# A two-layer hybrid decoder on one core: two down units' inner activations made in the last up pass, another order of layer 0's down passes, and one more slot

## The chip, the core and the metric

The kernel runs on one core of a Trainium2 chip. The core has five engines that each follow an instruction queue of their own: TensorE (PE, matmuls), VectorE (DVE), ScalarE (ACT), GpSimd (POOL) and SyncE (SP, which here only starts transfers). Transfers run on 16 DMA engines. The metric is the time in device microseconds (us) of one execution; lower is better.

## The reference

Two layers (DEPTH 2) on 1024 tokens of width 1024, in float32. Each layer is a mixer and a channel sub-layer, both with adaptive norms whose shifts, scales and gates come from a product of one vector with a 1024x6144 matrix ("ada"):

```python
for l in range(DEPTH):
    mod = (cond @ w_ada[l] + b_ada[l])[:, None, :]
    shift_a, scale_a, gate_a, shift_f, scale_f, gate_f = jnp.split(mod, N_MOD, axis=-1)
    h = rms_norm(x) * (1.0 + scale_a) + shift_a
    mix = hybrid_mixer(h, cos, sin, ...)   # 4 heads of gated linear attention, 4 of latent attention with rotary keys
    x = x + gate_a * mix
    h = rms_norm(x) * (1.0 + scale_f) + shift_f
    x = x + gate_f * (jnp.square(jax.nn.relu(h @ w_mlp_up[l])) @ w_mlp_down[l])
```

The two products of the channel sub-layer are 1024x1024x4096 (up) and 1024x4096x1024 (down).

## The kernel before

**Precision.** Each float32 operand is split into a high part (a cast on ACT, or on DVE) and a low part (the difference), and each product is three matmuls, high x high, high x low and low x high: L161 to L163 in `mm3`. In the channel sub-layer each is 128x128 by 512 columns.

**Up and down as seven products.** Each of the two big products is cut into 2x2 blocks and done by Strassen's scheme with seven products instead of eight (`PRODUCTS`). A product names one or two weight blocks, one or two activation blocks, and the result blocks that it is added to. A *pass* is one product; a pass has eight *units* g = 0..7 of 24 matmuls. `UP_ORDER` and `DOWN_ORDER[l]` fix the order of the passes; layer 0's down order is 4, 7, 1, 5, 6, 2, 3, layer 1's is 4, 7, 1, 5, 3, 2, 6. Products 1, 6 and 7 have two weight blocks and two activation blocks. In the down products, 4 and 3 have one weight block and two activation blocks, 5 and 2 two weight blocks and one activation block.

**What a unit needs.** Its weights are loaded by SP (L292, and L298 for a second block), added on DVE if there are two blocks (L304), cast on ACT (L307), and the low part is taken on DVE (L308). Its inner activations are added on DVE (L1289, in place when the block is used for the last time), cast on ACT (L1291), and the low part is taken on DVE (L1292); this is `combine`, called by `down_moving`. So a unit with two blocks on both sides costs DVE four operations of 128x1024. In some units of layer 0 a step of the ada product of a later use runs on DVE too (L256, one load of 512 KB each). At the end of an up unit its result is added to one or two of the blocks C (L1338, on DVE, from PSUM); when a block of C is complete, ACT squares its positive part (L1311, L1312; block (0,1) in the first down pass). At the end of a down pass four banks are added to x, four or eight operations on DVE (L1417).

**Slots.** All large tiles, weights raw and split, inner activations, C, x and so on, are slots of 128x1024 float32 from one pool of `NSLOT` = 51. Free slots are handed out first in, first out. Weights are prepared two units ahead and loaded up to one or two further units ahead, while at least eight slots are free (`get`); inner activations are made one unit ahead in the first two down passes and two units ahead after (`moving_ahead`).

**Order on an engine.** A scheduler, which runs when the program is built, decides where each instruction stands in its engine's queue, with the order of the code as a preference. So an operation can stand well ahead of its place in the code when its inputs are there; each engine then follows its queue strictly.

**Rotary tables.** Cosines and sines (`cosT`, `sinT`, with the gains `grp`, three permanent tiles) are made in layer 0's mixer. In each layer `rope_tables` makes two slots of tables from them: six POOL multiplications (L577, L578, L580) and two on DVE (L579). In layer 1 this stands at the mixer's start, where the last down pass of layer 0 ends; L431 to L433 there are the norm of the first half of the tokens.

**Start.** The constants (L178), then 14 smaller transfers, all issued on ACT's queue, the last of them the gain rows (L204) that the transpose L208 needs; the condition vector and all of ada hang on it.

## Time and profile before

| | us |
|---|---|
| median of 3 runs | 2353.1 (2352.49 to 2366.69) |
| the profiled execution, its own time | 2356.47 |
| its span (first to last instruction) | 2354.4 |
| PE busy | 2236.2 (95%) |
| DVE busy | 1810.4 (77%) |
| ACT busy | 1141.1 (48%) |
| POOL busy | 453.5 (19%) |

"Span" is the time from the first instruction to the last; 2.1 us lie around it. Stretches are given in us from the span's start. The mean granted clock of PE was 0.982 of full speed. Layer 0's up passes end at 880.9, its down passes at 1214.4; layer 1's up passes end at about 2025.

### The profile page before, as it was taken

To read this page: it belongs to the slowest core of one execution; us is meant where nothing else is said; L and a number is where in the kernel's file an instruction comes from. 1 tells how busy PE (TensorE), PEld (TensorE's weight loads), DVE (VectorE), ACT (ScalarE), POOL (GpSimd) and SP (SyncE) were. 2 spreads that over 40 slices of the span, in tenths; PEclk is the share of its full clock that TensorE was granted. 3 is DMA by queue.
4 is the path that set the end of the run, shared out by engine and by line. 5 is a ranking of instruction groups with operands and counts; after the bars stand their busy time and mean duration, and the time that the engine had idled before them with its cause. 6 is when DMAs were issued, how large, how long until landed. Compare 5 with 4: busy or idle time off the path is not lost.

```text
span 2354.4 us, 30787 instructions
## 1 busy us (share of the span) xinstructions
PE 2236.2 (95%) x11784; PEld 1897.1 (81%) x11784; DVE 1810.4 (77%) x2453; ACT 1141.1 (48%) x1764; POOL 453.5 (19%) x326
## 2 busy tenths in 40 slices
PE   6999999899999998998989999899999999999999
PEld 4788888788788876887878889788888878887887
DVE  5897867857888888989995757786674767877894
ACT  3364746534732383433444556575366217733432
POOL 2452642420030000000063355333102000000000
PEclk8999999999999999999999999999999999999999
DMA  9633100136668655765641211003454564375562
GB/s 345 205 97 99 55 27 10 46 125 212 199 206 274 217 167 174 249 225 197 239 131 45 70 51 41 10 10 100 144 169 124 180 202 146 110 237 189 163 212 81
DMA packets 244855, 340.51 MB, mean 145 GB/s; under 512 B 11078, under 2 KB 166884, under 8 KB 244708
## 3 DMA queue, kind: packets, MB, share of 16 engines
q1 hardware_dynamic: 244160, 338.08, 44.2%
q8 instruction: 92, 1.51, 0.3%
q10 hardware_dynamic: 548, 0.48, 0.1%
q14 instruction: 55, 0.45, 0.1%
HBM read 317.54 MB, written 20.97 MB: 144 GB/s over the span
## 4 chain that ended last, share of the span: by engine, by line
PE 63%; DVE 12%; DMA 7%; ACT 2%; issue 2%; POOL 1%; SPq 0%; DVEq 0%; ACTq 0%; POOLq 0%
PE ps_m L162 8%; PE ps_m L163 7%; PE ps_m L161 7%; PE ps_s L162 5%; PE ps_s L163 5%; PE ps_s L161 5%; PE ps_g L163 4%; PE ps_g L162 4%; PE ps_g L161 4%; DMA s<-in_w_mlp_down_dram 3%; PE ps_x L163 2%; PE ps_x L162 2%; PE ps_x L161 2%; DMA s<-in_w_mlp_up_dram 2%; DMA s<-in_w_ada_dram 1%
## 5 line engine op out<-in xcount | busy, mean ns | idle before, releaser
L307 ACT CAST s<-s 128x1024 fp32r<-128x1024 f32 (+2 forms) x306 | 315.2, 1035 | 465.5 <-DVE s L304 275.7
L162 PE MATMUL ps_m<-s,s 128*128 128x512 f32 (+3 forms) x1084 | 411.1, 380 | 15.2 <-DVE s L1292 14.2
L308 POOL TENSOR_TENSOR s<-s,s 128x1024 fp32r<-128x1024 f32 (+2 forms) x90 | 222.7, 2481 | 1044.9 <-DVE s L307 524.1
L161 PE MATMUL ps_m<-s,s 128*128 128x512 f32 (+3 forms) x1084 | 408.6, 381 | 8.6 <-ACT s L1291 5.4
L163 PE MATMUL ps_m<-s,s 128*128 128x512 f32 (+3 forms) x1084 | 408.3, 377 | 0.2 <-DVE s L308 0.2
L308 DVE TENSOR_TENSOR s<-s,s 128x1024 fp32r<-128x1024 f32 (+1 forms) x224 | 272.5, 1227 | 55.6 <-ACT s L307 47.6
L161 PE MATMUL ps_s<-s,s 128*128 128x512 f32 (+5 forms) x800 | 306.4, 387 | 6.6 <-ACT s L724 6.1
L163 PE MATMUL ps_s<-s,s 128*128 128x512 f32 (+5 forms) x800 | 305.3, 383 | 1.5 <-DVE s L308 1.5
L162 PE MATMUL ps_s<-s,s 128*128 128x512 f32 (+5 forms) x800 | 305.2, 382 | 0.5 <-DVE s L748 0.5
L304 DVE TENSOR_TENSOR s<-s,s 128x1024 f32<-128x1024 f32 x160 | 196.9, 1233 | 122.1 <-DMA s<-in_w_mlp_up_dram 77.6
L162 PEld LDWEIGHTS ps_m<-s,s 128*128 128x128 f32 x1084 | 206.4, 190 | 55.9 <-DVE s L1292 17.7
L161 PEld LDWEIGHTS ps_m<-s,s 128*128 128x128 f32 x1084 | 205.6, 190 | 46.5 <-ACT s L1291 7.4
L1291 ACT CAST s<-s 128x1024 fp32r<-128x1024 f32 x140 | 146.7, 1051 | 192.8 <-DVE s L1289 57.2
L163 PEld LDWEIGHTS ps_m<-s,s 128*128 128x128 f32 x1084 | 206.0, 190 | 35.8 <-DVE s L308 0.6
L162 PE MATMUL ps_g<-s,s 128*128 128x512 f32 (+1 forms) x506 | 195.0, 386 | 1.6 <-DVE s L1292 1.6
L161 PE MATMUL ps_g<-s,s 128*128 128x512 f32 (+1 forms) x506 | 194.6, 388 | 0.8 <-DVE s L1338 0.8
L163 PE MATMUL ps_g<-s,s 128*128 128x512 f32 (+1 forms) x506 | 194.3, 387 | 0.8 <-DVE s L308 0.8
L1292 DVE TENSOR_TENSOR s<-s,s 128x1024 fp32r<-128x1024 f32 x140 | 173.5, 1244 | 13.8 <-ACT s L1291 10.8
L161 PEld LDWEIGHTS ps_s<-s,s 128*128 128x128 f32 x800 | 150.8, 189 | 37.0 <-ACT s L724 8.7
L163 PEld LDWEIGHTS ps_s<-s,s 128*128 128x128 f32 x800 | 151.4, 189 | 30.9 <-DVE s L308 1.9
L162 PEld LDWEIGHTS ps_s<-s,s 128*128 128x128 f32 x800 | 151.6, 190 | 27.6 <-DVE s L748 0.7
L162 PE MATMUL ps_x<-s,s 128*128 128x512 f32 (+3 forms) x362 | 124.1, 344 | 0.0
(332 smaller groups left out, 4412.6 us busy)
## 6 DMA issues: line engine op xcount, KB each, us to landing
s<-in_w_mlp_up_dram SPq DMA_DIRECT2D x192, 512.0 KB, 4.9
s<-in_w_mlp_down_dram SPq DMA_DIRECT2D x192, 512.0 KB, 4.3
s<-in_w_ada_dram SPq DMA_DIRECT2D x80, 512.0 KB, 4.8
s<-in_w_in_dram SPq DMA_DIRECT2D x48, 512.0 KB, 3.9
s<-in_w_ada_dram SPq DMA_DIRECT2D x32, 256.0 KB, 4.6
xd<-s SPq DMA_DIRECT2D x16, 512.0 KB, 6.1
s<-in_w_out_dram SPq DMA_DIRECT2D x16, 512.0 KB, 4.5
s<-xd SPq DMA_DIRECT2D x16, 512.0 KB, 3.5
```

Source lines behind the costliest of these rows:

```text
L161: PE.matmul(o, lh, rh, start=start, stop=False)
L162: PE.matmul(o, lh, rl, start=False, stop=False)
L163: PE.matmul(o, ll, rh, start=False, stop=stop)
L304: V.tensor_tensor(raw[:, :n], raw[:, :n], u.second[:, :n], op=ALU.add if u.sign > 0 else ALU.subtract)
L307: (V.tensor_copy if u.eng[-2] == "v" else S.copy)(R(u.hi[:, :n]), raw[:, :n])
L308: (V if u.eng[-1] == "v" else G).tensor_tensor(R(u.lo[:, :n]), raw[:, :n], u.hi[:, :n], op=ALU.subtract)
L1291: S.copy(R(hi), t)
L1292: V.tensor_tensor(R(lo), t, hi, op=ALU.subtract)
```

## The change

1. In the last of the seven up passes (n = 6), after unit 3, the inner activations of down unit 0 are made, and after unit 6 those of down unit 1, in both layers. `down_moving`, `steps` and `moving_ahead` move ahead of the up loop for this.
2. Layer 0's down order becomes 4, 6, 7, 1, 5, 2, 3. The third pass, too, now makes inner activations only one unit ahead and loads weights only one further unit ahead (n < 3 where it was n < 2), in both layers.
3. `NSLOT` becomes 52. Room for it comes from small tiles and from the three permanent rotary tiles: in layer 0 both layers' tables are made, those of layer 1 are stored to DRAM (two transfers of 512 KB), and layer 1 loads them (two more) in place of making them.
4. The constants are loaded in two parts with the causal mask going elsewhere, so ACT's queue issues two more transfers ahead of the gain rows.

```diff
-NSLOT = 51
+NSLOT = 52
-DOWN_ORDER = ((4, 7, 1, 5, 6, 2, 3), (4, 7, 1, 5, 3, 2, 6))
+DOWN_ORDER = ((4, 6, 7, 1, 5, 2, 3), (4, 7, 1, 5, 3, 2, 6))
...
-    cs = cp.tile([P, 416], F32, name="cs")
-    nc.scalar.dma_start(cs, cst[:, 0:416])
+    cs = cp.tile([P, 288], F32, name="cs")
+    nc.scalar.dma_start(cs[:, 0:128], cst[:, 0:128])
+    nc.scalar.dma_start(cs[:, 128:288], cst[:, 256:416])
...
     nc.scalar.dma_start(lvf[:, 0:320], cst[:, 416:736])
+    nc.scalar.dma_start(lvf[:, 320:448], cst[:, 128:256])
...
     def rope_angles():
-        ang = AR.alloc()
+        ang, trig = AR.alloc(), AR.alloc()
+        cosT, sinT, grp = trig[:, 0:256], trig[:, 256:512], trig[:, 512:768]
...
+        rope_tables(1, trig)
+        for i in range(2):
+            nc.sync.dma_start(rope_dram[i], rope_slots[i])
+        AR.free(*rope_slots)
+        rope_tables(0, trig)
+        AR.free(trig)
...
     def rope_tables(l, trig):
...
+            if trig is None:
+                nc.sync.dma_start(rope_slots[i], rope_dram[i])
+                continue
...
+        steps = [(m, g) for m in down_order for g in range(8)]
+        made = {}
+
+        def moving_ahead(i):
+            for j in steps[:i + 1]:
+                if j not in made:
+                    made[j] = down_moving(*j)
...
+                if n == 6 and g in (3, 6):
+                    moving_ahead(g // 6)
...
-                get(u, 2, 1 if n < 2 else 2)
-                moving_ahead(n * 8 + g + (1 if n < 2 else 2))
+                get(u, 2, 1 if n < 3 else 2)
+                moving_ahead(n * 8 + g + (1 if n < 3 else 2))
```

Line numbers shift with the change: L304, L308 become L307, L311; L256 becomes L259; L1289, L1292 become L1302, L1305; L1338 becomes L1370; L1417 becomes L1433; L431, L433 become L434, L436.

How it moves instructions, at three places. **First**, DVE where layer 0's up passes end. Before, the last two additions to C (the rows from PSUM tile ps_m at the head) stand ahead of everything that down unit 0 needs except its first addition; the low part of unit 0 is s_786, of unit 1 s_789, of unit 2 s_795, and the in-place additions (a tile added to itself) are for the pass of product 7:

```order
L1338 TENSOR_TENSOR s_747_7798<-s_747_7798,ps_m 128x512
L1338 TENSOR_TENSOR s_532_6077<-s_532_6077,ps_m 128x512
L1289 TENSOR_TENSOR s_494_5853<-s_494_5853,s_495_5855 128x1024
L308 TENSOR_TENSOR s_791_8211<-s_783_8170,s_790_8210 128x1024
L1292 TENSOR_TENSOR s_786_8175<-s_784_8172,s_785_8174 128x1024
L1289 TENSOR_TENSOR s_487_5809<-s_487_5809,s_488_5811 128x1024
L1292 TENSOR_TENSOR s_789_8181<-s_787_8178,s_788_8180 128x1024
L1289 TENSOR_TENSOR s_800_8257<-s_501_5897,s_553_6259 128x1024
L1292 TENSOR_TENSOR s_795_8219<-s_793_8216,s_794_8218 128x1024
```

Now unit 0's addition and low part (s_768, s_770) stand among the additions to C of the middle of that pass, with an in-place addition for product 7 between them:

```order
L1302 TENSOR_TENSOR s_768_7979<-s_481_5744,s_539_6112 128x1024
L1370 TENSOR_TENSOR s_725_7568<-s_725_7568,ps_s 128x512
L1370 TENSOR_TENSOR s_498_5837<-s_498_5837,ps_s 128x512
L1302 TENSOR_TENSOR s_481_5744<-s_481_5744,s_482_5746 128x1024
L1370 TENSOR_TENSOR s_725_7568<-s_725_7568,ps_g 128x512
L1370 TENSOR_TENSOR s_498_5837<-s_498_5837,ps_g 128x512
L1305 TENSOR_TENSOR s_770_7982<-s_768_7979,s_769_7981 128x1024
```

and behind the last two additions to C comes unit 2's low part (s_798), then unit 3's (s_805):

```order
L1370 TENSOR_TENSOR s_750_7780<-s_750_7780,ps_m 128x512
L1370 TENSOR_TENSOR s_535_6059<-s_535_6059,ps_m 128x512
L1302 TENSOR_TENSOR s_497_5835<-s_497_5835,s_498_5837 128x1024
L311 TENSOR_TENSOR s_794_8193<-s_792_8164,s_793_8192 128x1024
L1305 TENSOR_TENSOR s_798_8201<-s_796_8198,s_797_8200 128x1024
L259 SCALAR_TENSOR_TENSOR s_759_7896<-s_799_8230,cond,s_759_7896 128x1024
L1302 TENSOR_TENSOR s_803_8239<-s_504_5879,s_556_6241 128x1024
L311 TENSOR_TENSOR s_801_8234<-s_795_8196,s_800_8233 128x1024
L1302 TENSOR_TENSOR s_809_8296<-s_516_5933,s_568_6297 128x1024
L1302 TENSOR_TENSOR s_504_5879<-s_504_5879,s_505_5881 128x1024
L1305 TENSOR_TENSOR s_805_8242<-s_803_8239,s_804_8241 128x1024
```

Two units (four DVE operations) moved from behind the last addition to C to ahead of it; the in-place additions for product 7 stay on both sides.

**Second**, DVE in layer 0's second down pass. Before, this is product 7, whose activation additions were done in the first pass, so a unit has two weight rows (L304, L308) and one low part (L1292):

```order
L1292 TENSOR_TENSOR s_848_8547<-s_487_5809,s_847_8546 128x1024
L308 TENSOR_TENSOR s_840_8490<-s_837_8484,s_839_8489 128x1024
L304 TENSOR_TENSOR s_849_8574<-s_849_8574,s_850_8576 128x1024
L304 TENSOR_TENSOR s_843_8536<-s_843_8536,s_844_8538 128x1024
L1292 TENSOR_TENSOR s_854_8585<-s_494_5853,s_853_8584 128x1024
L304 TENSOR_TENSOR s_855_8612<-s_855_8612,s_856_8614 128x1024
L308 TENSOR_TENSOR s_846_8542<-s_843_8536,s_845_8541 128x1024
```

Now it is product 6. A unit has its own addition (s_858), its low part (s_860), two weight rows, and beside them an in-place addition (s_725) for product 3, the last pass:

```order
L1302 TENSOR_TENSOR s_858_8567<-s_551_6199,s_725_7568 128x1024
L311 TENSOR_TENSOR s_850_8525<-s_847_8519,s_849_8524 128x1024
L307 TENSOR_TENSOR s_854_8558<-s_854_8558,s_855_8560 128x1024
L1302 TENSOR_TENSOR s_725_7568<-s_725_7568,s_498_5837 128x1024
L1305 TENSOR_TENSOR s_860_8570<-s_858_8567,s_859_8569 128x1024
```

So a unit of the second pass has five rows on DVE where it had three.

**Third**, DVE where layer 0's last down pass ends and layer 1's mixer starts. Before, the two rotary rows (L579) stand between the norm and the additions that empty the last pass's banks:

```order
L433 SCALAR_TENSOR_TENSOR s_1124_10246<-tmp,mod,s_1124_10246 128x512
L433 SCALAR_TENSOR_TENSOR s_1125_10251<-tmp,mod,s_1125_10251 128x512
L579 SCALAR_TENSOR_TENSOR s_1181_10808<-sinT,grp 128x8x32 x2
L1417 SCALAR_TENSOR_TENSOR s_994_9411<-ps_m,mod,s_994_9411 128x512
L1417 SCALAR_TENSOR_TENSOR s_941_9073<-ps_m,mod,s_941_9073 128x512
```

Now nothing stands between; one more weight cast (L310) stands among the norm's rows, some way ahead:

```order
L434 SCALAR_TENSOR_TENSOR tmp<-s_832_8396,mod,tmp 128x512
L436 SCALAR_TENSOR_TENSOR s_1127_10228<-tmp,mod,s_1127_10228 128x512
L436 SCALAR_TENSOR_TENSOR s_1128_10233<-tmp,mod,s_1128_10233 128x512
L1433 SCALAR_TENSOR_TENSOR s_1053_9713<-ps_m,mod,s_1053_9713 128x512
L1433 SCALAR_TENSOR_TENSOR s_889_8729<-ps_m,mod,s_889_8729 128x512
```

Two rows have gone from ahead of the additions; POOL's six rows of layer 1's tables have gone too and stand in layer 0's mixer, beside layer 0's own six.

## Rows read from the trace of the kernel before

**Rows 1.** The page, busy time of each engine (share of the span, instructions).
```profile
PE 2236.2 (95%) x11784; PEld 1897.1 (81%) x11784; DVE 1810.4 (77%) x2453; ACT 1141.1 (48%) x1764; POOL 453.5 (19%) x326
```

**Rows 2.** Windows: start:end, length, busy PE PEld DVE ACT POOL, PEclk, DMA.
```profile
680.00:720.00 40.00, 40.00 (x178) 33.14 (x177) 35.80 (x43) 8.43 (x8) 5.70 (x3) 1.00 0.77 244
880.00:920.00 40.00, 31.30 (x128) 24.56 (x127) 33.72 (x38) 18.84 (x19) 0.00 (x0) 0.87 0.39 131
1080.00:1120.00 40.00, 34.71 (x144) 27.91 (x142) 38.48 (x37) 15.84 (x16) 0.00 (x0) 0.91 0.59 203
1200.00:1240.00 40.00, 33.52 (x212) 30.75 (x211) 32.99 (x31) 16.50 (x23) 23.12 (x12) 0.91 0.44 141
2120.00:2160.00 40.00, 35.16 (x147) 28.61 (x146) 31.00 (x29) 15.86 (x16) 0.00 (x0) 0.91 0.58 199
```

**Rows 3.** Waits in 870:930: who waited for whom, total us, times, longest.
```profile
PE ps_m L161 <- ACT s L1291: 4.7, 1, 4.7
...
PE ps_m L162 <- DVE s L1292: 2.6, 1, 2.6
...
PE ps_m L161 <- DVE s L1338: 1.4, 1, 1.4
```

**Rows 4.** DVE's timeline at the turn: start, us, operation, xcount [idle before].
```profile
881.17 2.35 DVE L1289 TENSOR_TENSOR s<-s,s 128x1024 f32<-128x1024 f32 x2
...
886.91 1.27 DVE L1338 TENSOR_TENSOR s<-s,ps_m 128x512 f32<-128x512 f32 x2
...
889.25 1.21 DVE L308 TENSOR_TENSOR s<-s,s 128x1024 fp32r<-128x1024 f32 x1
890.38 1.21 DVE L1292 TENSOR_TENSOR s<-s,s 128x1024 fp32r<-128x1024 f32 x1
```

**Rows 5.** DVE by line in 881:1214: xcount | busy us, mean ns | idle before.
```profile
L304 DVE TENSOR_TENSOR s<-s,s 128x1024 f32<-128x1024 f32 x40 | 48.7, 1222 | 11.5 <-DMA s<-in_w_mlp_down_dram 10.4 <-issue 0.8
...
L256 DVE SCALAR_TENSOR_TENSOR s<-s,cond,s 128x1024 f32<-128x1024 f32 x15 | 19.2, 1283 | 12.7 <-DMA s<-in_w_ada_dram 12.7
```

**Rows 6.** Waits in 1030:1130, the largest of PE.
```profile
PE ps_m L162 <- DVE s L1292: 5.4, 3, 4.6
```

**Rows 7.** Waits in 1190:1225, the only one of PE.
```profile
PE ps_m L609 <- ACT s L404: 6.5, 1, 6.5
```

**Rows 8.** DVE's timeline where layer 1's mixer starts.
```profile
1197.59 5.07 DVE L431 SCALAR_TENSOR_TENSOR tmp<-s,mod,tmp 128x512 f32<-128x512 f32 x3
...
1203.90 0.74 DVE L431 SCALAR_TENSOR_TENSOR tmp<-s,mod,tmp 128x512 f32<-128x512 f32 x1
...
1217.64 1.80 DVE L579 SCALAR_TENSOR_TENSOR s<-sinT,grp 128x256 f32<-128x256 f32 x2
1219.37 2.71 DVE L1417 SCALAR_TENSOR_TENSOR s<-ps_m,mod,s 128x512 f32<-128x512 f32 x4
```

**Rows 9.** POOL's timeline at the same place, first and last of four table operations.
```profile
1194.32 1.07 POOL L577 TENSOR_TENSOR s<-cosT,grp 128x256 f32<-128x256 f32 x1
...
1198.12 1.18 POOL L578 TENSOR_TENSOR s<-cosT,grp 128x256 f32<-128x256 f32 x1
```

**Rows 10.** The start, timeline of ACT's queue of transfers (ACTq).
```profile
0.77 0.39 ACTq L178 DMA_DIRECT2D cs<-in_cst_dram  x1
...
13.13 0.91 ACTq L204 DMA_DIRECT2D tmp<-in_k_norm_nope_dram  x2
```

**Rows 11.** The start, timeline of PE: the transpose that waits for the gain rows.
```profile
16.23 0.45 PE L208 MATMUL ps_x<-cs,tmp 128*128 128x128 f32 x1 [5.62 <-DMA tmp<-in_k_norm_nope_dram]
```

**Rows 12.** POOL's timeline in layer 0's mixer: last table, first operation that uses them.
```profile
117.30 0.73 POOL L578 TENSOR_TENSOR s<-cosT,grp 128x256 f32<-128x256 f32 x1
122.84 0.61 POOL L881 COPY s<-s 128x128 f32<-128x128 f32 x1 [4.82 <-DVE s L865]
```

**Rows 13.** Layer 1's down passes: waits in 2050:2135, the largest for a transfer.
```profile
DVE s L304 <- DMA s<-in_w_mlp_down_dram: 10.9, 5, 5.2
```

**Rows 14.** SP's own waits in 2040:2140, the longest.
```profile
SPq L292 <- PE ps_s L163: 35.4, 6, 11.8
```

More of the change, by code (lines that the diff above doesn't have):

```diff
@@ L176, in hybrid_kernel @@
     S.preload_act_table_set("natural_log_exp_and_others")
-    cs = cp.tile([P, 416], F32, name="cs")
-    nc.scalar.dma_start(cs, cst[:, 0:416])
+    cs = cp.tile([P, 288], F32, name="cs")
+    nc.scalar.dma_start(cs[:, 0:128], cst[:, 0:128])
+    nc.scalar.dma_start(cs[:, 128:288], cst[:, 256:416])
     ident = cs[:, 0:128]
-    invf = cs[:, 256:288]
-    m_even = cs[:, 288:352]
-    m_odd = cs[:, 352:416]
+    invf = cs[:, 128:160]
+    m_even = cs[:, 160:224]
+    m_odd = cs[:, 224:288]
     lvm = cp.tile([P, 320], U8, name="lvm")
@@ L185, in hybrid_kernel @@
     nc.scalar.dma_start(lvf[:, 0:320], cst[:, 416:736])
+    nc.scalar.dma_start(lvf[:, 320:448], cst[:, 128:256])
     V.tensor_copy(lvm, lvf[:, 0:320])
     bfc = cp.tile([P, 256], BF16, name="bfc")
-    V.tensor_copy(bfc, cs[:, 0:256])
+    V.tensor_copy(bfc[:, 0:128], ident)
+    V.tensor_copy(bfc[:, 128:256], lvf[:, 320:448])
     ident_bf, causal_bf = bfc[:, 0:128], bfc[:, 128:256]
@@ L218, in hybrid_kernel @@
     cond = cp.tile([P, 8], F32, name="cond")
-    ct = sp.tile([P, 8], F32, tag="c8", name="ct")
-    ct2 = sp.tile([P, 8], F32, tag="c8", name="ct2")
+    ct = tmp()[:, 0:8]
+    ct2 = tmp()[:, 0:8]
     cT = colsv[:, 96:104]
@@ L452, in evac_split @@
         V.scalar_tensor_tensor(R(dst_lo), ps, gain, dst_hi, op0=ALU.mult, op1=ALU.subtract)
-    ssq0 = sp.tile([P, 8], F32, tag="ssq0", name="ssq0")
-    rst0 = sp.tile([P, 8], F32, tag="rst0", name="rst0")
+    ssq0 = cp.tile([P, 8], F32, name="ssq0")
+    rst0 = cp.tile([P, 8], F32, name="rst0")
     xT = x0T = []
@@ L523, in rope_angles @@
         V.tensor_copy(posf, posi)
-        posT = sp.tile([P, 8], F32, tag="posT", name="posT")
+        posT = cp.tile([P, 8], F32, name="posT")
         ps = bank("x")
@@ L568, in rope_angles, with rope_tables @@
         AR.free(ang)
-    def rope_tables(l):
+        rope_tables(1, trig)
[4 more added lines that the diff above has]
+        AR.free(trig)
+    def rope_tables(l, trig):
         rope_slots[:] = [AR.alloc(), AR.alloc()]
+        if trig is not None:
+            cos3, sin3 = (trig[:, i * 256:i * 256 + 256].rearrange("p (t f) -> p t f", t=8) for i in range(2))
+            grp = trig[:, 512:768]
         for i in range(2):
@@ L1146, in layer_mixer @@
                     rope_angles()
-                rope_tables(l)
+                else:
+                    rope_tables(l, None)
             elif kind == "E":
@@ L1278, in hybrid_kernel @@
         AR.free(*xT)
-        ngate = sp.tile([P, 8], F32, tag="ngate", name="ngate")
+        ngate = cp.tile([P, 8], F32, name=f"ngate{l}")
         hq = {(r, c): hs[c][r] for r in range(2) for c in range(2)}
@@ L1312, in square_relu, with down_moving @@
             S.activation(c, c, AF.Square)
+        down_order = DOWN_ORDER[l]
+        down_uses = {b: sum(b in PRODUCTS[m][1][:2] for m in down_order) for b in C}
+        def down_moving(m, g):
+            one, two, sign = PRODUCTS[m][1]
+            if g == 0:
+                for b in (one, two):
+                    if b is not None:
+                        down_uses[b] -= 1
+            return combine(C[one][g], C[two][g] if two else None, sign, down_uses[one] == 0, two is not None and down_uses[two] == 0)
+        steps = [(m, g) for m in down_order for g in range(8)]
[4 more added lines that the diff above has]
+                    made[j] = down_moving(*j)
         moving = up_moving(UP_ORDER[0])
@@ L1352, in hybrid_kernel @@
         tail = l + 1 == DEPTH
-        down_order = DOWN_ORDER[l]
         acc = None
-        uses = {b: sum(b in PRODUCTS[m][1][:2] for m in down_order) for b in C}
         finals = {b: [m for m in down_order if b in [x for x, _ in PRODUCTS[m][2]]][-1] for b in C}
@@ L1358, in hybrid_kernel @@
         xv = lambda d, c, xs=xs: xs[d // 4, c][d % 4 // 2][:, d % 2 * 512:d % 2 * 512 + 512]
-        def down_moving(m, g):
-            one, two, sign = PRODUCTS[m][1]
-            if g == 0:
-                for b in (one, two):
-                    if b is not None:
-                        uses[b] -= 1
-            return combine(C[one][g], C[two][g] if two else None, sign, uses[one] == 0, two is not None and uses[two] == 0)
         def store_out(c, r, tags):
@@ L1378, in store_out @@
                 AR.free(ob)
-        steps = [(m, g) for m in down_order for g in range(8)]
-        made = {}
-        def moving_ahead(i):
-            for j in steps[:i + 1]:
-                if j not in made:
-                    made[j] = down_moving(*j)
         for n, m in enumerate(down_order):
```

10 lines of the change are left out of this document (3 added, 7 removed).

## Prediction

> **What bounds the kernel now.** I read the page's busy times first: PE is busy for 2236.2 of 2354.4 us [rows 1], so only some 118 us of idle time, and what a lower clock costs, are there to be had. Then the windows, by 40 us, to find where PE stands still. In a stretch of the channel sub-layers without a stall PE runs 178 matmuls in 40 us [rows 2], so one takes 0.225 us and a unit of 24 takes 5.4 us. Four of the five windows of rows 2 are that one and the three stalls that this change can reach: at the turn from up to down in layer 0 (880 to 920) 128 matmuls, 50 short, which is 11.2 us; in layer 0's down passes (1080 to 1120) 34 short, 7.6 us; in layer 1's down passes (2120 to 2160) 31 short, 7.0 us. The fourth stall is at the start of layer 1's mixer, where matmuls of another size run, so that I read it from a wait: 6.5 us [rows 7].
>
> Then the waits. At the turn PE waits three times, 8.7 us together [rows 3]: for unit 0's high part, for a bank, for its low part. The other 2.5 of the 11.2 us are matmuls at the lower clock (granted 0.87 there, where the undisturbed window has 1.00 [rows 2]). DVE's timeline shows why: it runs without a gap, ends the last addition to C at 888.2, and has spent its time between on additions for units that come much later; unit 0's low part starts only at 890.38 [rows 4]. The stall at 1080 is the same kind, PE waiting for a low part of DVE [rows 6]. So in these passes **DVE is the engine to count**: it follows its queue strictly, one 128x1024 operation every 1.14 us (889.25 to 890.38 in rows 4), a bank addition every 0.66 us, an ada step every 1.20 us.
>
> **The turn and layer 0's first two down passes.** What the edit says: two units (two additions, two low parts, 4.6 us of DVE) are made before the up pass ends. The order shows that they displace other rows rather than lengthen the pass: the last 46 DVE rows up to the last addition to C were 28 additions to C, 6 ada steps, 6 weight lows and 6 activation additions (37.7 us); now they are 28, 5, 6, 5 and the two activation lows (37.6 us). So the last addition to C should end at 888.2 again, with units 0 and 1 ready by then and PE supplied until 880.9 + 10.8 = 891.7. Unit 2's low part is three rows behind (888.2 + 3.4 = 891.6): in time. The 8.7 us of waits at the turn go.
>
> But what follows is heavier. From the last addition to C to the low part of unit 13 (the sixth of product 6) DVE now has 53 operations of 1.14 us (23 activation additions, 12 activation lows, 11 weight lows, 7 weight additions), six ada rows, eight bank additions and a few small ones: 73.9 us, so 962.1. Eleven of the 23 additions are in-place ones for products 7 and 3, which nobody needs yet. PE would want unit 13 at 880.9 + 13 x 5.4 = 951.1. So PE loses 11, or about 10, since a unit's first matmuls need its high part only, in pieces of 1 to 3 us. Before, the second pass was product 7, its additions already made, and DVE had 38.0 us of work between the ends of the first and second pass; now 44.8. So this term is 11.2 gone and some 10 new, and where DVE is behind, its waits for transfers begin to count: they were 10.4 + 12.7 us in the seven passes [rows 5], 3.3 a pass. I take **0**. Bounds: -8 (the new pieces cost a quarter) and +12 (half of the 23 us fall in these two passes and reach PE).
>
> **Layer 0's later passes.** Between the ends of consecutive passes DVE had, from the third to the sixth, 39.5, 43.0, 44.3 and 43.0 us of work, against 43.1 us of PE per pass: the third of these is where the 7.6 us are lost, the waits of rows 5 on top. Now it is 38.0, 41.8, 39.8 and 41.2, nine us less, since product 6 with its two additions no longer follows product 5 with its eight bank additions, and the additions for 7 and 3 lie behind. With 3.3 us of waits a pass the fourth still overruns a little. I take **-6**; bounds -9 and 0.
>
> **The start of layer 1's mixer.** PE waits for banks that DVE empties from 1219.37 on, and the two rotary rows stand right ahead, 1.80 us [rows 8]; they go, and a cast of about 0.7 us comes among the rows ahead. POOL's four cosine rows run from 1194.32 to 1199.3 [rows 9]; beside POOL three of DVE's L431 take 5.07 us, where one alone takes 0.74 [rows 8], 2.8 us too long, with POOL's weight lows as partner for part of it. I give 2 us to the tables. Sum **-3.1**; bounds -6.5 (the whole wait [rows 7]) and -1.1. The two loads in their place lie some 70 us ahead of their first use.
>
> **Layer 0's mixer** gets those operations: six on POOL at 0.73 us, 4.4 us, and two on DVE. POOL is idle for 4.82 us between the last table and the first use [rows 12], so POOL covers it; without that cover it is 4.4. DVE's two rows (0.9 each, as in rows 8) and its slowing beside POOL are not covered: **+1.0**; bounds 0 and +6.
>
> The page SBUF — State Buffer of the Trainium skill, section Who interferes with whom, speaks against this part: a DVE instruction with two SBUF inputs and a POOL instruction that reads SBUF lock each other out for the whole instruction. By it the six rows would cost DVE up to 4.4 us in layer 0, the sum +6.2 rather than +1.0 there, and give back 5.0 rather than 2 in layer 1. The slowed L431 of rows 8 point the same way, but no row shows a full lock-out.
>
> **The start.** Transfers on ACT's queue gate the transpose L208 [rows 11]. Two more stand ahead: each costs between its issue, 0.39 us, and the queue's mean spacing, (14.04 - 0.77) / 15 = 0.88 us [rows 10]. The condition vector, and so ada and the first norm, are late by that: **+1.3**; bounds 0 (hidden behind weight loads) and +1.8.
>
> **Layer 1's down passes.** The order of products stays. DVE waits 10.9 us there for weights [rows 13] because SP's issues wait for slots [rows 14]. One slot more lets each load go about 0.7 us earlier (some eight slots turn over per 5.4 us), 3.4 us over five waits; half of it reaches PE: **-1.5**. The third pass loads one unit less ahead, which can take it back; bounds -7.0 (the stall goes) and +4. The turn in layer 1 had no stall, so the early units bring nothing there; the cover is DVE's free time, since no ada runs there.
>
> **Sum.** 0 - 6 - 3.1 + 1.0 + 1.3 - 1.5 = **-8.3 us**. The profiled execution took 2356.47, span 2354.4; that becomes 2348.2. It stands 3.4 above the median of the runs, so for the median 2353.1 - 8.3 = **2344.8**, say 2345. The order inside the mixers shifts as well with the slots; I have no sign for it, and put 5 us either way into the range.
>
> **Rivals.** *All stalls open* (12%): the in-place additions fill gaps of DVE and delay nothing, since before, too, eight of them stood at the turn and PE ran on. Then the turn gives 10, the later passes 7.6, layer 1 5, the mixer 3.1, less 2.3: 2330. Against it: at the turn DVE had no gap [rows 4].
> *DVE's waits take over, slower* (15%): product 6 with two blocks on both sides now comes while DVE is behind, with ada loads in the pass before, so each wait of DVE for a transfer reaches PE. Half of the 23.1 us of rows 5 cost +11.6, and the sum is +3.3: 2356; all of it gives 2368. It decides from 8.3 us on. For it: L256 alone waited 12.7 us; against: a DVE that is late finds its loads landed.
> *Stalls only move* (20%): the ten us lost in the first passes push the later ones too, and the gain of six is not there: 2352.
> *Full lock-out of DVE by POOL* (5%): layer 0's six rows hold DVE for all of their 4.4 us, with the rest 5.2 more than I took, and layer 1 gives back 3 more, since the rows leave there: 2347. It is the rule of the Trainium skill's page SBUF — State Buffer, section Who interferes with whom, told above.
> The forecast (48%) covers 2338 to 2351.
>
> **Numbers.** Range 2331 to 2360: it takes in the forecast, moved stalls, most of the slower rival and the edge of the open one. About 1% is what a measurement of this kernel can tell from no change, here 23.5 us: faster than 2329.6 needs nearly all stalls open, 8%; slower than 2376.6 needs more than all of DVE's waits, 3%; within 89%.
>
> **What would show it.** After: no wait near 880.9 above 2 us, and short waits of PE for L1305 (the low part) in 890 to 975; fewer than 50 but more than 30 matmuls lost there. The wait of 4.6 us at 1085 gone, and no window of the later passes under 170. The wait at layer 1's mixer start near 3.5 us. L208 about a microsecond later. I am wrong if the first two passes run at 178 matmuls per 40 us (then the count of DVE's rows is no guide), or if DVE's waits for transfers there exceed 10 us.

## The result, and the profile after

The changed kernel takes **2372.1 us** (median of 6 runs, 2368.9 to 2376.7). The ratio to the kernel before is **1.0072, 95% interval 1.0049 to 1.0094**: about 17 us slower by the ratio (19 between the medians of 2353.1 and 2372.1), where I had forecast 8 faster (2345, range 2331 to 2360). It is less than the 1% that the prediction called distinguishable, but its sign is clear.

The busy times hardly change, PE 10 us more than in [rows 1] for the same instructions:

```profile
PE 2246.2 (95%) x11784; PEld 1910.6 (81%) x11784; DVE 1814.8 (77%) x2454; ACT 1138.3 (48%) x1764; POOL 455.2 (19%) x326
```

To see where the time went I cut both traces at the same DVE rows: the first and the last addition to C in each layer, and the first addition of the last pass's banks to x (in layer 1 the last of those four). In the trace after, layer 0's three cuts are these (start, us, operation):

```profile
633.36 0.68 DVE L1370 TENSOR_TENSOR s<-s,ps_s 128x512 f32<-128x512 f32 x1
...
913.18 1.27 DVE L1370 TENSOR_TENSOR s<-s,ps_m 128x512 f32<-128x512 f32 x2
...
1246.72 1.41 DVE L1433 SCALAR_TENSOR_TENSOR s<-ps_m,mod,s 128x512 f32<-128x512 f32 x2
```

The stretches between the cuts, in us (profiled executions):

| | start and mixer, layer 0 | up 0 | down 0 | mixer, layer 1 | up 1 | down 1 |
|---|---|---|---|---|---|---|
| before | 617.0 | 270.6 | 331.9 | 548.1 | 262.5 | 317.4 |
| after | 633.4 | 280.4 | 332.9 | 548.9 | 257.9 | 310.4 |
| difference | **+16.4** | **+9.8** | +1.0 | +0.8 | -4.6 | -7.0 |

So the loss of 26 us lies ahead of the first down pass, where my sum had +2.3, and the gain lies in layer 1's channel sub-layer, where I had 1.5. The windows of after that answer to [rows 2], and the one with the new stall of the up passes, whose row of before comes first (start:end, length, busy PE PEld DVE ACT POOL, granted clock, DMA):

```profile
760.00:800.00 40.00, 40.00 (x182) 33.23 (x181) 34.60 (x40) 9.02 (x9) 0.00 (x0) 1.00 0.80 260
```

and after:

```profile
760.00:800.00 40.00, 33.09 (x134) 25.91 (x133) 28.75 (x31) 8.15 (x8) 0.00 (x0) 0.91 0.69 217
880.00:920.00 40.00, 40.00 (x178) 33.15 (x177) 39.25 (x48) 35.95 (x39) 0.00 (x0) 1.00 0.47 154
920.00:960.00 40.00, 36.10 (x162) 29.06 (x160) 37.86 (x40) 12.26 (x12) 0.00 (x0) 1.00 0.72 249
960.00:1000.00 40.00, 38.84 (x158) 30.27 (x159) 40.00 (x38) 13.72 (x13) 0.00 (x0) 0.96 0.48 157
1000.00:1040.00 40.00, 31.94 (x124) 25.52 (x123) 25.82 (x25) 13.12 (x13) 0.00 (x0) 0.87 0.59 198
1080.00:1120.00 40.00, 40.00 (x178) 33.15 (x177) 37.01 (x36) 17.30 (x17) 0.00 (x0) 1.00 0.64 208
2120.00:2160.00 40.00, 40.00 (x178) 33.14 (x177) 37.11 (x35) 16.38 (x16) 0.00 (x0) 1.00 0.64 217
```

The turn (880 to 920) now runs at the full 178 matmuls, 1080 and 2120 too. In layer 0's second down pass 36 matmuls are lost (920 to 1000), in the third 54, and in the up passes 48 (134, where the same window of before had 182).

**The stall in the up passes.** PE's and DVE's timelines: a transpose of the ada product waits for an ada step, which stands on DVE behind weight additions that wait for their loads. The 48 matmuls, at 40/178 = 0.225 us each, come to some 11 us (an estimate from these rows): about the whole +9.8 of the stretch. The granted clock of the window is 0.91, where before it was 1.00.

```profile
790.97 1.94 PE L266 MATMUL ps_x<-cs,s 128*128 128x128 f32 x8 [4.70 <-DVE s L259]
```
```profile
775.08 1.23 DVE L307 TENSOR_TENSOR s<-s,s 128x1024 f32<-128x1024 f32 x1 [4.84 <-DMA s<-in_w_mlp_up_dram]
...
786.67 2.36 DVE L307 TENSOR_TENSOR s<-s,s 128x1024 f32<-128x1024 f32 x2 [3.87 <-DMA s<-in_w_mlp_up_dram]
...
789.55 1.28 DVE L259 SCALAR_TENSOR_TENSOR s<-s,cond,s 128x1024 f32<-128x1024 f32 x1
```

**The down passes of layer 0.** PE waits twice for the low part in the second pass and twice for a weight in the third; the latter two stand behind loads that DVE waits for (PE's timeline; then DVE's of the third pass):

```profile
960.22 0.51 PE L162 MATMUL ps_g<-s,s 128*128 128x512 f32 x1 [4.09 <-DVE s L1305]
968.53 0.50 PE L162 MATMUL ps_g<-s,s 128*128 128x512 f32 x1 [0.94 <-DVE s L1305]
1005.58 1.22 PE L161 MATMUL ps_m<-s,s 128*128 128x512 f32 x2 [2.94 <-ACT s L310]
1027.81 0.79 PE L161 MATMUL ps_m<-s,s 128*128 128x512 f32 x1 [5.13 <-ACT s L310]
```
```profile
1003.23 1.23 DVE L307 TENSOR_TENSOR s<-s,s 128x1024 f32<-128x1024 f32 x1 [2.97 <-DMA s<-in_w_mlp_down_dram]
1023.18 1.23 DVE L307 TENSOR_TENSOR s<-s,s 128x1024 f32<-128x1024 f32 x1 [3.54 <-DMA s<-in_w_mlp_down_dram]
```

**The start.** The gain rows' transpose is 1.7 us later than in [rows 11], but the ada product 6.6 us (20.3 before, 26.9 now). In DVE's queue a cast of mixer weights (L310), which waits for its load, now stands ahead of the condition vector:

```profile
25.98 0.69 DVE L310 CAST s<-s 128x1024 fp32r<-128x1024 f32 x1 [4.55 <-DMA s<-in_w_in_dram]
26.58 0.15 DVE L398 SCALAR_TENSOR_TENSOR rs_a<-rs_y 128x4 f32<-128x4 f32 x1
26.66 0.16 DVE L230 TENSOR_TENSOR cond<-colsv,tmp 128x8 f32<-128x8 f32 x1
```

Before, the cast stood behind all of these:

```profile
20.00 0.17 DVE L227 TENSOR_TENSOR cond<-colsv,ct 128x8 f32<-128x8 f32 x1
...
25.62 0.69 DVE L307 CAST s<-s 128x1024 fp32r<-128x1024 f32 x1 [4.45 <-DMA s<-in_w_in_dram]
```

**Theories.** A: the loss is the start's and the reordering that the 52nd slot brings; the edits of the channel sub-layers gain. B: the rotary tables made in layer 0 cost its mixer. C: the edits of the channel sub-layers slow the up passes.

### The profile page after: what moved, and what is told of

It reads as the page before. It is cut to its first block, busy times and chain, and to the rows that moved or that the text cites. A ratio compares the mean times of both kernels' runs of the same rounds, so it can differ in the third digit from the quotient of the medians.

```text
span 2370.9 us, 30824 instructions
## 1 busy us (share of the span) xinstructions
PE 2246.2 (95%) x11784; PEld 1910.6 (81%) x11784; DVE 1814.8 (77%) x2454; ACT 1138.3 (48%) x1764; POOL 455.2 (19%) x326
## 3 DMA queue, kind: packets, MB, share of 16 engines
q1 hardware_dynamic: 244736, 340.18, 43.9%
## 5 line engine op out<-in xcount | busy, mean ns | idle before, releaser
L310 ACT CAST s<-s 128x1024 fp32r<-128x1024 f32 (+2 forms) x306 | 315.3, 1035 | 533.3 <-DVE s L307 272.5
L311 POOL TENSOR_TENSOR s<-s,s 128x1024 fp32r<-128x1024 f32 (+2 forms) x90 | 221.9, 2477 | 1070.7 <-ACT s L310 868.4
L311 DVE TENSOR_TENSOR s<-s,s 128x1024 fp32r<-128x1024 f32 (+1 forms) x224 | 272.0, 1217 | 56.1 <-ACT s L310 46.9
L162 PE MATMUL ps_s<-s,s 128*128 128x512 f32 (+5 forms) x800 | 305.9, 383 | 0.0
L307 DVE TENSOR_TENSOR s<-s,s 128x1024 f32<-128x1024 f32 x160 | 204.5, 1279 | 107.1 <-DMA s<-in_w_mlp_up_dram 66.4
L1305 DVE TENSOR_TENSOR s<-s,s 128x1024 fp32r<-128x1024 f32 x140 | 173.4, 1243 | 11.2 <-ACT s L1304 5.9
L1302 DVE TENSOR_TENSOR s<-s,s 128x1024 f32<-128x1024 f32 x100 | 123.1, 1236 | 9.8 <-PE ps_x L163 4.0
```

The source lines that it names most:

```text
L162: PE.matmul(o, lh, rl, start=False, stop=False)
L307: V.tensor_tensor(raw[:, :n], raw[:, :n], u.second[:, :n], op=ALU.add if u.sign > 0 else ALU.subtract)
L310: (V.tensor_copy if u.eng[-2] == "v" else S.copy)(R(u.hi[:, :n]), raw[:, :n])
L311: (V if u.eng[-1] == "v" else G).tensor_tensor(R(u.lo[:, :n]), raw[:, :n], u.hi[:, :n], op=ALU.subtract)
L1302: V.tensor_tensor(t, one, two, op=ALU.add if sign > 0 else ALU.subtract)
L1305: V.tensor_tensor(R(lo), t, hi, op=ALU.subtract)
```

## The experiments

All runs in one table. Ratios are to the kernel before, run again beside each group of runs, where its median was 2355.3 to 2359.7, so between groups the ratio compares better than the medians. The stretches are those above, from one profiled execution of each run; "to up 0" is start and mixer of layer 0.

| run | median us | ratio (95%) | to up 0 | up 0 | down 0 | mixer 1 | up 1 | down 1 |
|---|---|---|---|---|---|---|---|---|
| e1 | 2353.8 | 0.998 (0.9959, 1.0001) | 616.4 | 271.1 | 336.4 | 551.4 | 264.0 | 305.9 |
| e2 | 2349.9 | 0.9973 (0.9957, 0.9989) | 617.2 | 271.1 | 332.5 | 547.3 | 263.0 | 306.7 |
| e3 | 2355.7 | 0.9988 (0.9976, 1.0001) | 619.5 | 269.8 | 328.4 | 548.5 | 260.8 | 317.8 |
| e4 | 2369.8 | 1.0045 (1.0023, 1.0067) | 628.8 | 279.9 | 329.9 | 548.5 | 258.0 | 310.3 |
| e5 | 2393.5 | 1.0163 (1.0148, 1.0178) | 614.2 | 283.7 | 362.1 | 558.5 | 258.5 | 309.7 |
| e6 | 2349.7 | 0.9979 (0.9969, 0.9989) | 614.4 | 278.4 | 333.6 | 544.3 | 257.9 | 310.3 |
| e7 | 2354.5 | 0.9993 (0.9981, 1.0006) | 631.7 | 274.9 | 323.0 | 546.3 | 257.9 | 310.4 |
| e8 | 2347.9 | 0.9966 (0.9954, 0.9977) | 621.4 | 270.4 | 331.4 | 551.5 | 257.9 | 310.6 |
| e9 | 2360.4 | 1.0002 (0.9988, 1.0016) | 614.6 | 271.1 | 343.4 | 551.0 | 262.6 | 308.8 |
| e10 | 2336.0 | 0.9899 (0.9877, 0.992) | 614.2 | 270.1 | 321.2 | 549.7 | 265.0 | 305.8 |
| e11 | 2350.3 | 0.996 (0.9946, 0.9975) | 612.2 | 278.5 | 328.9 | 550.4 | 257.9 | 310.6 |
| e12 | 2363.8 | 1.0023 (1.0006, 1.004) | 618.3 | 271.8 | 338.9 | 550.7 | 264.0 | 312.9 |
| e13 | 2362.8 | 1.0019 (1.0003, 1.0036) | 633.3 | 279.4 | 327.5 | 545.4 | 257.9 | 310.6 |
| e14 | 2346.4 | 0.9956 (0.9935, 0.9977) | 619.4 | 272.6 | 326.3 | 545.8 | 265.8 | 307.3 |
| e15 | 2334.6 | 0.9913 (0.9883, 0.9942) | 613.9 | 272.8 | 322.6 | 545.4 | 257.9 | 310.9 |

**e1**, the kernel before with parts 1 and 2 of the change, 51 slots.

```diff
-DOWN_ORDER = ((4, 7, 1, 5, 6, 2, 3), (4, 7, 1, 5, 3, 2, 6))
+DOWN_ORDER = ((4, 6, 7, 1, 5, 2, 3), (4, 7, 1, 5, 3, 2, 6))
...
+                if n == 6 and g in (3, 6):
+                    moving_ahead(g // 6)
...
-                get(u, 2, 1 if n < 2 else 2)
+                get(u, 2, 1 if n < 3 else 2)
```

> The kernel before with the two edits of the channel sub-layers alone: early inner activations, layer 0's other down order and the third pass's shorter lookahead; 51 slots, old rotary tables, old start. DVE's order in the mixers and in the first six up passes is then that of before. Theory A (the loss sits in the start and in the reordering that the 52nd slot brings): the stretch to the first addition to C stays at 617, layer 0's up passes at 270 to 271, and the whole ends between 2340 and 2353. Theory C (the edits of the channel sub-layers make the up passes slower): layer 0's up passes take about 280, the whole 2360 or more.

 Layer 0's start, mixer and up passes are those of before to a microsecond. C falls. The whole ends just above A's range, level with the kernel before: layer 1's down passes gain 11.5 us, layer 0's lose 4.5.

**e2**, the changed kernel with one edit.

```diff
-NSLOT = 52
+NSLOT = 51
```

> The changed kernel with 51 slots in place of 52 (rotary tables in DRAM and the split load of the constants stay). Theory A: the mixers' order is again that of before but for the start and the tables, so only the start's 5 to 7 us are lost: the first addition to C near 623, layer 0's up passes 270 to 271, the whole between 2343 and 2358. Theory B (the rotary tables made in layer 0 cost its mixer some ten us): the first addition to C near 633 as with 52 slots.

 A holds and B falls: with the same tables and the same start the first addition to C is at 617, earlier even than A's 623, and the whole is 22 us faster than with 52 slots. The start's loss is there (ada at 27.9) and is not to be seen 590 us later: in this kernel a late start costs less than equal queues scatter (614 to 621 us, see below). The mixers' stretches of 51 and of 52 slots:

```profile
28.00:617.00 589.00, 549.44 (x3394) 479.79 (x3388) 460.17 (x762) 313.13 (x604) 208.63 (x159) 0.97 0.37 121
```
```profile
27.00:633.00 606.00, 556.79 (x3390) 485.03 (x3390) 458.30 (x762) 313.32 (x605) 210.52 (x159) 0.95 0.36 117
```

The first is e2, the second the changed kernel. The matmuls are the same (a few records are missing), and DVE, ACT and POOL are busy for as long. PE stands still for 49.2 us in place of 39.6, and is busy 7.3 us longer at a granted clock of 0.95 for 0.97.

**e3**, the kernel before with parts 3 and 4 alone, but 51 slots.

```diff
-    cs = cp.tile([P, 416], F32, name="cs")
+    cs = cp.tile([P, 288], F32, name="cs")
...
+        rope_tables(1, trig)
+        for i in range(2):
+            nc.sync.dma_start(rope_dram[i], rope_slots[i])
...
```

> The kernel before with the room made (rotary tables in DRAM, small tiles moved, split load), but 51 slots and none of the edits of the channel sub-layers. Theory A: start +5 to +7, a wait of about 3 us gone at layer 1's mixer, the rest as before: 2353 to 2360. Theory B: 2363 or more, the first addition to C near 633.

 A's figure, and again nothing for B. PE's wait at layer 1's mixer goes from 6.5 us [rows 7] to 3.3:

```profile
PE ps_m L621 <- ACT s L407: 3.3, 1, 3.3
```

**e4**, the changed kernel, the two additional transfers behind the condition vector.

```diff
-    nc.scalar.dma_start(cs[:, 128:288], cst[:, 256:416])
-    nc.scalar.dma_start(lvf[:, 320:448], cst[:, 128:256])
-    V.tensor_copy(bfc[:, 128:256], lvf[:, 320:448])
...
+    nc.scalar.dma_start(cs[:, 128:288], cst[:, 256:416])
+    nc.scalar.dma_start(lvf[:, 320:448], cst[:, 128:256])
+    V.tensor_copy(bfc[:, 128:256], lvf[:, 320:448])
     ropeC, ropeS, rope_slots = [None, None], [None, None], []
```

> The changed kernel, 52 slots, with its two additional transfers of constants moved behind the condition vector; the cast of the first mixer weights then stands behind the condition vector on DVE again. Theory A: the ada product starts near 20.3 again instead of 26.9, the first addition to C about 3 to 7 us earlier than 633, the whole 2365 to 2369. If the stretch has slack the 6.6 us vanish before the first addition to C and the whole stays at 2372.

 The edit missed: another cast that waits for a load, that of the late mask itself, now stands ahead of the condition vector, and the ada product starts at 25.6.

```profile
24.20 0.23 DVE L513 CAST bfc<-tmp 128x128 bf16<-128x128 f32 x1 [5.00 <-DMA tmp<-in_cst_dram]
...
25.32 0.17 DVE L227 TENSOR_TENSOR cond<-colsv,tmp 128x8 f32<-128x8 f32 x1
```

So it tells nothing on the start's price with 52 slots; the 628.8 stay those of 52 slots.

**e5**, the changed kernel with 50 slots.

```diff
-NSLOT = 52
+NSLOT = 50
```

> The changed kernel with 50 slots. Theory R (it is the rotation: slots are reused first in, first out, so any other count gives every later tile another slot, another earlier tile to wait for, and the scheduler another order, good or bad): layer 0's mixer and up passes differ from those of 51 slots by several us, in either direction, and the whole lies 5 us or more from the 2350 of 51 slots. Theory F (one more slot lets the scheduler move work ahead that holds up more urgent work): fewer slots do no such harm, the stretch to the first addition to C stays within 3 us of 617, and only the passes that wait for slots get longer.

 F's figure for the mixer is met, though it doesn't show F's mechanism, and R's hardly: 614.2 lies among the mixers of 51 slots, although by the line of code only 66% of its rows on DVE stand in the sequence of e2. So another order is not a slower one by itself. In the up passes (283.7) R's figure is met. Compared with e2, everything behind the mixer is longer but layer 1's channel sub-layer taken whole, layer 0's down passes by 30 us, the whole by 44; DVE's waits there at L307 for loads are 45.2 us, in e2 18.6 (DVE by line, 898 to 1260):

```profile
L307 DVE TENSOR_TENSOR s<-s,s 128x1024 f32<-128x1024 f32 x40 | 48.8, 1223 | 45.5 <-DMA s<-in_w_mlp_down_dram 45.2
```

**e6 and e8**, the 52nd slot handed out late: from layer 0's channel sub-layer on (e6), or layer 1's (e8, with `l == 1`).

```diff
     AR = Arena(ap_, NSLOT)
+    AR.free_list.remove(NSLOT - 1)
...
+        if l == 0:
+            AR.free_list.append(NSLOT - 1)
         ngate = cp.tile([P, 8], F32, name=f"ngate{l}")
```

> The changed kernel, in which the 52nd slot is handed out only from layer 0's channel sub-layer on: the mixer of layer 0 runs in the order of 51 slots, the up passes behind it nearly in that of 52. If the up passes' loss comes from their own order, the first addition to C is near 617 again and layer 0's up passes still take 278 to 281: the whole 2354 to 2362. If they were slow only because the mixer before ended differently, they take 271, and the whole is 2350 or less.

> The changed kernel, in which the 52nd slot is handed out only from layer 1's channel sub-layer on. Everything ahead is in the order of 51 slots: first addition to C near 617, layer 0's up passes near 271, layer 1's mixer near 547. What is left is the slot's effect in layer 1's channel sub-layer: up passes about 258 in place of 263, down passes about 310 in place of 307, so 2346 to 2350 in all.

 Each stage goes with its own slot count: in e6 the mixer is that of 51 slots, the up passes (278.4) those of 52; in e8 only layer 1 is that of 52, where it is even (5 us better in the up passes, 4 worse in the down passes). e8's whole is as expected; e6's lies 4 us under its range, by mixers of 614 and 544.

**e7**, the changed kernel, the two rules on free slots raised by one.

```diff
-        while ustate["pos"] < min(n, len(units)) and len(AR.free_list) >= 5:
+        while ustate["pos"] < min(n, len(units)) and len(AR.free_list) >= 6:
...
-        while ustate["loaded"] < min(i + 1 + look + loads, len(units)) and len(AR.free_list) >= 8:
+        while ustate["loaded"] < min(i + 1 + look + loads, len(units)) and len(AR.free_list) >= 9:
```

> The changed kernel, 52 slots, with the two rules that look at free slots raised by one (weights prepared ahead while 6 are free, loaded ahead while 9 are), so that as many units are loaded ahead as with 51. If it is the lookahead that the 52nd slot changes, mixer and up passes go back to 617 and 271 and the whole to about 2350. If it is the rotation, the first addition to C stays at 630 to 634, the up passes stay over 275, and the whole at 2365 or more.

 The mixer stays at 631.7, and up to the first addition to C its queue on DVE is, line by line, that of the changed kernel: there the two rules decide nothing, and the loss is not what they let load ahead. Whether it is the rotation or, as theory F has it, work moved ahead, no run separates. But up passes (274.9) and down passes (323.0) gain, which neither theory had: with less ahead they are shorter in this run.

**e9 to e12** take the edits of the channel sub-layers apart, on e2. e9:

```diff
-                if n == 6 and g in (3, 6):
-                    moving_ahead(g // 6)
```

> The changed kernel with 51 slots and without the two early units. If these units are what ends the stall at layer 0's turn, about 8 us of waits return there. Layer 1's down passes took 306.7 us with 51 slots against 317.4 before: if the early units brought that, they take 314 to 318 again; if the third pass's shorter lookahead brought it, they stay at 306 to 309. Whole 2355 to 2362 in the first case, 2350 to 2355 in the second.

 Layer 0's down passes lose 10.9 us, with the three waits of the turn [rows 3] back:

```profile
PE ps_m L161 <- ACT s L1304: 5.1, 1, 5.1
PE ps_m L162 <- DVE s L1305: 2.6, 1, 2.6
PE ps_m L161 <- DVE s L1370: 1.0, 1, 1.0
```

In layer 1 the early units bring only 2 us, little more than the scatter there (305.8 to 307.3 in e1, e2, e10 and e14).

e10, on e2:

```diff
-DOWN_ORDER = ((4, 6, 7, 1, 5, 2, 3), (4, 7, 1, 5, 3, 2, 6))
+DOWN_ORDER = ((4, 7, 1, 5, 6, 2, 3), (4, 7, 1, 5, 3, 2, 6))
```

> The changed kernel with 51 slots and layer 0's old down order (4, 7, 1, 5, 6, 2, 3); the early units and the third pass's shorter lookahead stay. Theory A (the new order makes DVE the bound in the second pass, which takes away what the turn gave): the turn's 11 us stay gone, no stall of 4 to 5 us in the second pass, the old stall in the fifth pass is back, layer 0's down passes 320 to 326 in place of 332.5, the whole 2338 to 2345. Rival (the stalls only move whatever the order): 330 to 336, the whole 2348 or more.

 As A had it: 321.2 in place of 332.5; the whole ends 2 us under A's range. This version beats both kernels, by 1.0% and 1.7%. The first two passes lose 3.8 us of waits at low parts, the fifth still has the old stall of [rows 6] (PE's waits, 884 to 975, then 1050 to 1100):

```profile
PE ps_m L162 <- DVE s L1305: 2.0, 2, 1.3
PE ps_g L162 <- DVE s L1305: 1.8, 1, 1.8
```
```profile
PE ps_m L162 <- DVE s L1305: 5.1, 2, 4.6
```

e11 is e6 with the two rules of e7 from the same place on.

```diff
+            AR.spare = 1
...
-len(AR.free_list) >= 5:
+len(AR.free_list) >= 5 + AR.spare:
...
```

> The changed kernel, the 52nd slot handed out only from layer 0's channel sub-layer on, and from there the two rules on free slots raised by one. It puts together what the stages showed: first addition to C near 614, up passes 275, down passes 323, layer 1's mixer 546, up passes 258, down passes 310: 2326 to the last bank addition, 2334 to 2340 in all, faster than both kernels. If the orders of the stages depend on what ran before, the gain of the thresholds in the down passes is lost and it stays near 2350.

 A miss, 10 us above the range: up 278.5 and down 328.9, and the whole is no faster than e6. e7's gain in the up passes is not there, though the rules are the same: the gains of single stages did not add.

e12:

```diff
-                get(u, 2, 1 if n < 3 else 2)
-                moving_ahead(n * 8 + g + (1 if n < 3 else 2))
+                get(u, 2, 1 if n < 2 else 2)
+                moving_ahead(n * 8 + g + (1 if n < 2 else 2))
```

> The changed kernel with 51 slots, the third down pass with its old, longer lookahead (weights two further units ahead, activations two). If the shorter lookahead is what opened layer 1's down passes, they go from 306.7 back to 313 to 318 and the whole to 2356 or more; if the early units did it, they stay at 306 to 309, and the whole within 4 us of 2350.

 Layer 1's down passes go from 306.7 to 312.9 and layer 0's from 332.5 to 338.9; layer 1's stall in the third pass is back, 4.4 us where [rows 2] lost 31 matmuls:

```profile
2137.33 0.51 PE L162 MATMUL ps_m<-s,s 128*128 128x512 f32 x1 [4.36 <-DVE s L1305]
```

So the shorter lookahead, which I had only feared, is worth about 6 us in each layer: in layer 1 clear of the scatter, in layer 0 less so, where the same edits gave 331.4 (e8) to 336.4 (e1).

**e13 to e15** ask how much of it depends on what else. e13 is e10 with 52 slots.

```diff
-NSLOT = 51
+NSLOT = 52
```

> The changed kernel (52 slots) with layer 0's old down order alone. If the 52nd slot's cost is a matter of the order of the mixer and the up passes and has nothing to do with the down order, the first addition to C is at 628 to 634 and layer 0's up passes take 278 to 281, as in the changed kernel, and the whole is 14 to 24 us over the 2336 of 51 slots with the same order: 2350 to 2360. If the slot was only bad together with the new down order, it is 2336 to 2342.

 27 us slower than e10 (its expectation ended at 24), with mixer and up passes as in the changed kernel, and a stall at the same place of the up passes (PE's waits, 755 to 805):

```profile
PE ps_x L266 <- DVE s L259: 4.2, 1, 4.2
```

The slot's price does not hang on the down order.

e14 is the kernel before with only early units and the shorter third lookahead.

```diff
+                if n == 6 and g in (3, 6):
+                    moving_ahead(g // 6)
...
-                get(u, 2, 1 if n < 2 else 2)
+                get(u, 2, 1 if n < 3 else 2)
```

> The kernel before with nothing but the two early units and the third pass's shorter lookahead: 51 slots, old rotary tables, old start, old down order. If the room made for the slot is worth nothing by itself, as the run of that part alone showed (2355.7), layer 0's down passes take 320 to 326, layer 1's 304 to 308, and the whole 2335 to 2342. If the rotary tables in DRAM carry part of the gain, it is 2343 or more.

 2346.4: ten more than e10, so the room made for the slot is worth more beside these edits than alone (e3). About half lies ahead of the first addition to C, where equal queues scatter by as much; as much again is the wait at layer 1's mixer, 10.0 us with the tables made there against 5.1 in e10:

```profile
PE ps_m L609 <- ACT s L404: 10.0, 1, 10.0
```
```profile
PE ps_m L621 <- ACT s L407: 5.1, 1, 5.1
```

e15 is e8 with the diff of e10.

> 51 slots with layer 0's old down order, early units and shorter third lookahead, and the 52nd slot only from layer 1's channel sub-layer on. By the stages: as with 51 slots and the old order (2336) up to 1755, then up passes 258 for 265 and down passes 310 for 306: 2331 to 2336.

 As expected, and not to be told from e10.

**What settles it.** Nine kernels with room made and 51 slots in layer 0's mixer (e2, e3, e6, e8 to e12, e15) reach the first addition to C at 612.2 to 621.4 us, seven of them with the same queue on DVE up to there (613.9 to 621.4, the scatter of equal queues); four with 52 (changed, e4, e7, e13) at 628.8 to 633.4. The nine average 616.2; the three with the old start and the old tables (before, e1, e14) 617.6, so neither costs anything there that shows.

In the up passes DVE's waits for transfers at L307 and L259 and the length go together: 23.6 us and 271.1 (e2), 32.3 and 274.9 (e7), 34.1 and 278.4 (e6), 37.9 and 280.4 (changed). DVE by line, e2 and then the changed kernel:

```profile
L307 DVE TENSOR_TENSOR s<-s,s 128x1024 f32<-128x1024 f32 x32 | 41.3, 1293 | 14.2 <-DMA s<-in_w_mlp_up_dram 14.2
L259 DVE SCALAR_TENSOR_TENSOR s<-s,cond,s 128x1024 f32<-128x1024 f32 x27 | 37.4, 1384 | 9.4 <-DMA s<-in_w_ada_dram 9.4
```
```profile
L307 DVE TENSOR_TENSOR s<-s,s 128x1024 f32<-128x1024 f32 x32 | 42.1, 1322 | 23.0 <-DMA s<-in_w_mlp_up_dram 22.9
L259 DVE SCALAR_TENSOR_TENSOR s<-s,cond,s 128x1024 f32<-128x1024 f32 x27 | 36.0, 1332 | 15.2 <-DMA s<-in_w_ada_dram 15.0
```

All ten kernels with 51 slots there, the kernel before among them, take 269.8 to 272.8; all six with 52 (also e4, e11, e13) take 274.9 to 280.4, and in each of the six PE waits once for an ada step, 2.1 us in e11 and 4.1 to 4.7 in the others. Only e5, with 50 slots, does not fit: 28.8 us of these waits, 283.7 us, and no such wait of PE. Why the order of 52 slots is the worse one in the mixer stays open: its waits of PE lie at other places, but no single one makes the ten us that PE stands still longer.

## Why the prediction was wrong

| step | forecast us (bounds) | measured |
|---|---|---|
| turn and first two down passes, layer 0 | 0 (-8 to +12) | +4.4 (93.4 to 97.8) |
| later passes, layer 0 | -6 (-9 to 0) | -3.4 (238.5 to 235.1) |
| wait at layer 1's mixer | -3.1 (-6.5 to -1.1) | -0.6 (6.5 to 5.9); -3.2 in e3 |
| start and layer 0's mixer | +2.3 | **+16.4** |
| layer 0's up passes | not in the sum | **+9.8** |
| layer 1's up passes | not in the sum | -4.6 |
| layer 1's down passes | -1.5 (-7 to +4) | -7.0 |

**The step that failed** is one sentence: "The order inside the mixers shifts as well with the slots; I have no sign for it, and put 5 us either way into the range." It was sized without looking, it speaks of the mixers alone, and the up passes had no term at all. What stood in its place: one edit, 51 to 52, costs 22 us by e2 and 27 by e13 against e10, some 16 to 19 of them in layer 0's mixer and 9 in its up passes. In the up passes the path is shown: weight additions that wait for their loads stand ahead of an ada step that PE needs; why these loads land later with 52 slots is not. In the mixer the slot is shown as the cause, and how it costs the time stays open.

The warning was in the front: free slots go first in, first out, so one more gives every later tile another predecessor to wait for, and the scheduler writes another queue. I read the queues at three places, at those that the edits name. They could have been read everywhere: only 52% of DVE's rows stand in the same sequence before and after, where with 51 slots (e2) 91% do (by the line of code, in the longest common pieces). That gives no sign, as e5's mixer shows, but it says that nothing measured before need hold in the other half, so a range of 5 us was not to be had from it.

**The start** was wrong as a mechanism: not the queue's spacing (1.7 us, near the 1.3 I took), but a cast ahead of the condition vector, visible in the order. It cost nothing at the end that shows (e2).

**The down passes of layer 0** went as the count of DVE's rows said. The turn's waits are gone (first pass 49.5 to 42.5), the second pass is 11.4 us longer (43.9 to 55.3, DVE without a gap from 960 to 1000, 36 matmuls lost where I had named 30 to 50), the stall of 4.6 us at 1085 is gone. The rows from the last addition to C to unit 13's low part take 76.7 us in the trace, where I had counted 73.9. The third pass, which I had counted at 38.0 us of DVE's work and so without a loss, has 8.1 us of PE's waits behind late loads; there the sign "no window of the later passes under 170" failed, with 124. That the new order takes back what the early units give is shown with 51 slots by e9 and e10: the units are worth 10.9 us, the order costs 11.3. With 52 slots (e13 against the changed kernel) the order costs 5.4.

**Layer 1's down passes**: right in kind (a stall that goes), wrong in cause and size. I gave it to the slot and called the shorter third lookahead a risk; it is for the most part that lookahead (e12: 6.2 us), and the slot costs 4 us there (e2 against the changed kernel). Where the other 4.5 us come from, 317.4 before to e12's 312.9, is not shown. The up passes' 4.6 us are the slot's (e8: 257.9, with 51 slots 263.0).

**The rivals.** None had the place. "DVE's waits take over, slower" had the sign and 15%, but its 2356 to 2368 were for the down passes, which came out even.

**The tables**: six POOL rows in layer 0's mixer cost nothing there to see (e3, 619.5 for 617.0 with the later start in it). My +1.0 for them was below the 1.8 us of its own two DVE rows. In layer 1's mixer PE's wait fell by 3.2 us in e3, as forecast, but in the changed kernel by 0.6, outside my bounds, and e2 and e10 wait 5.7 and 5.1 us too: the term is not borne out beside the other edits. The wait in the changed kernel:

```profile
PE ps_m L621 <- ACT s L407: 5.9, 1, 5.9
```

In the changed kernel weight lows of POOL stand beside DVE's norm where the tables stood; that they make the wait is not shown.

One sum of the rivals is off by a microsecond: "stalls only move" gives 2351 by its own terms, not 2352.

## What to carry to other kernels

Where slots or buffers rotate first in, first out and a scheduler writes the queues, as here, their number is an edit of the whole program: price it by a run of that number alone, ahead of the edits for which the room was wanted. Of a list of edits that come together, look in the new queues first for a row that waits for a transfer ahead of a row that others wait for, also where the edits have no business. Counting an in-order engine's rows per pass works where that engine is the bound: here it gave the turn and the second pass; it says nothing of loads that come late.
